# Paired order of the output tiles, and all operand and weight sums on VectorE, in a two-layer decoder trunk

## The chip, the cores and the metric

The kernel runs on one core of a Trainium2 chip. The time is the device time of one execution in microseconds (us). A core has five engines that run their own instructions in order and meet through semaphores: TensorE (PE in the rows, PEld its weight loads), VectorE (DVE), ScalarE (ACT), GpSimd (POOL) and SyncE (SP), which here issues the loads.

## The reference

The reference is a trunk of two pre-norm residual blocks on 512 tokens of width 1024. The first block's mixer is HGRN2 beside retention, the second's is native sparse attention; each mixer ends in an output projection, and each block ends in a SwiGLU layer of hidden width 2816. Cut to what matters here:

```python
for layer in range(2):
    x = x + mixer(rmsnorm(x, g_mix)) @ w_out
    y = rmsnorm(x, g_ffn)
    x = x + (silu(y @ w_gate) * (y @ w_up)) @ w_down
return rmsnorm(x, g_final)
```

Everything is float32.

## The kernel before

All activations lie transposed: the residual stream is eight tiles `h[m]`, each of 128 channels by 512 tokens. To keep float32 accuracy, every operand of a matmul is cut into a high part, cast by ScalarE to the fast fp32r format, and a low part, the rest, which VectorE subtracts; `mm3` then issues three matmuls (high by high, high by low, low by high). Weights are cut in `split` (wh at L77, wl at L78), everything else in `cut` (high at L213, low at L214). Raw weights come by DMA into a ring of three buffers, `raw`; a load is issued only when the tile three loads back has been read by all its readers.

`ffn` does the output projection of the mixer and the SwiGLU layer. First it makes the eight output tiles in the order m = 0 to 7. Each has its own PSUM tile `ps_o`, which TensorE fills by 24 matmuls; VectorE adds it to `h[m]` (L286); `token_side` then makes the operands from the scaled tile, and `square` adds its squares to `acc` for the norm.

The gate and up products follow a scheme of Strassen and Winograd over a 2x2 split of weights and tokens, with seven products for eight. The operands on the token side are b1 and b2 (b3), which are cuts of halves of the scaled tile, and four sums: t1 is the high half of the tokens less the low half, made from tiles 0 to 3 alone, and t3, t2, t4 combine tile m (4 to 7) with tile m − 4. On the weight side, `weight_side` makes four sums s1 to s4 (L259, L260, L262, L264) of the four 128x512 blocks a11, a12, a21, a22 of a hidden tile. There are 22 hidden tiles j per layer, made in groups of 2, 4, 4, 4, 4, 4, and each has its seven products, five reads of these from PSUM (L331, L336, L338, L340 on VectorE and copies on ScalarE), a scaling by the norm (L341 and L342 on GpSimd), the silu (L343), the product with up (L344) and its cut (L347, L348). Between the tiles of one group stand the down projections of the group before, whose results VectorE adds to `h` (L313).

In which order each engine runs its instructions is decided when the program is built: a scheduler simulates the engines and takes the instructions as they become ready. So a change of the engine of one instruction shifts its neighbours too.

GpSimd makes t1 of tiles 0 to 3, the three sums of tile 4, the adds to `acc` for tiles 1 to 4, and all weight sums; VectorE does the rest.

Of the kernel before, what the change touches and what calls it, by code (L numbers as in the profile page):

```python
# [13 lines left out]
ALU = mybir.AluOpType  # L14
# [5 lines left out]
TH = T // 2  # L20
D = 1024
KD = D // P
# [8 lines left out]
NHEAD = 16  # L31
START = "x0 f0 x1 x2 x3 f1 x4 q0 x5 x6 q1 x7"
WARM = 10
BANK_OUT = (0, 3)
OWN_DOWN = (0, 3, 6)
AHEAD = 4
# [15 lines left out]
class Core:  # L52
# [105 lines left out]
    def run(self):  # L158
        tc, nc, io = self.tc, self.nc, self.io
        with tc.tile_pool(name="sp", bufs=1) as sp, tc.tile_pool(name="wp", bufs=1) as wp, \  # L160
# [25 lines left out]
            ps = self.bank(0, "ps_w")  # L186
            for _ in range(WARM):
                nc.tensor.matmul(ps[:, :P], self.ones, self.ones, start=True, stop=True)
# [28 lines left out]
    def token_side(self, m, gain, kept, b):  # L217

        nc, fs = self.nc, self.fs
        g = self.par[:, C_GAIN + 8 * gain + m:C_GAIN + 8 * gain + m + 1]  # L220
        x = fs.tile([P, T], F32, tag=("g", "s", "xg")[min(m // 2, 2)], name="xg", bufs=2)
        nc.scalar.activation(x, self.h[m], AF.Identity, scale=g)
        lo, hi = x[:, :TH], x[:, TH:]
        tr = lambda: fs.tile([P, TH], F32, tag="tr", name="tr", bufs=7)
        if m < 4:
            b[1].append(self.cut("b1", lo, TH, 4))
            t1 = tr()
            nc.gpsimd.tensor_tensor(t1, hi, lo, ALU.subtract)
            b[5].append(self.cut("t1", t1, TH, 4))
            kept.append(x)  # L230
            return
        xh, xl = self.cut("b2", x, T, 4)
        b[2].append((xh[:, :TH], xl[:, :TH]))
        b[3].append((xh[:, TH:], xl[:, TH:]))
        y = kept[m - 4]
        t3, t2, t4 = tr(), tr(), tr()
        eng = nc.gpsimd if m == 4 else nc.vector
        eng.tensor_tensor(t3, hi, y[:, TH:], ALU.subtract)
        eng.tensor_tensor(t2, t3, y[:, :TH], ALU.add)
        eng.tensor_tensor(t4, lo, t2, ALU.subtract)  # L240
        b[7].append(self.cut("t3", t3, TH, 4))
        b[6].append(self.cut("t2", t2, TH, 4))
        b[4].append(self.cut("t4", t4, TH, 4))

    def weight_side(self, j, layer):

        nc, fs = self.nc, self.fs
        raw = []
        for i in range(2):
            w = self.wp.tile([P, WN], F32, tag="raw", name="raw", bufs=3)  # L250
            nc.sync.dma_start(w, self.io["gu"][layer, 2 * j + i])
            raw += [w[:, :WS], w[:, WS:]]
        a11, a12, a21, a22 = raw
        sw = lambda: fs.tile([P, WS], F32, tag="sw", name="sw", bufs=4)
        a = {}
        a[1], = self.split(a11, WS, False)
        a[2], = self.split(a12, WS, False)
        s1, s2, s3, s4 = sw(), sw(), sw(), sw()
        nc.gpsimd.tensor_tensor(s1, a21, a22, ALU.add)  # L259
        nc.gpsimd.tensor_tensor(s2, s1, a11, ALU.subtract)  # L260
        a[5] = self.cut("s", s1, WS, 5)
        nc.gpsimd.tensor_tensor(s3, a11, a21, ALU.subtract)  # L262
        a[6] = self.cut("s", s2, WS, 5)
        nc.gpsimd.tensor_tensor(s4, a12, s2, ALU.subtract)  # L264
        a[7] = self.cut("s", s3, WS, 5)
        a[4], = self.split(a22, WS, False)
        a[3] = self.cut("s", s4, WS, 5)
        return a

    def ffn(self, outs, w_out, gain, layer, next_gain):  # L270
        tc, nc, io, sp = self.tc, self.nc, self.io, self.sp
        with tc.tile_pool(name="fs", bufs=1) as fs, tc.tile_pool(name="fps", bufs=6, space=PSUM) as fps:
            self.fs = fs
            acc = sp.tile([P, T], F32, tag="acc", name="acc", bufs=1)
            b = {i: [] for i in range(1, 8)}
            kept = []
            for m in range(KD):
                ps = self.bank(self.turn + 1 + m // 3, "ps_o") if m in BANK_OUT else \
                    fps.tile([P, T], F32, tag="gu", name="ps_o")
                w = self.weight(w_out[m])  # L280
                if m == BANK_OUT[1] and self.last is not None:
                    with tc.issue_after(self.last):
                        self.dense_t(ps, w, outs)
                else:
                    self.dense_t(ps, w, outs)
                nc.vector.tensor_tensor(self.h[m], ps, self.h[m], ALU.add)  # L286
                self.token_side(m, gain, kept, b)
                self.square(m, self.h[m], acc, m < 5)

            def product(i, a, ps=None):  # L290

                new = ps is None
                if new:
                    ps = fps.tile([P, T], F32, tag="gu", name=f"p{i}")[:, :TH]
                ah, al = a[i]
                for k, (bh, bl) in enumerate(b[i]):
                    c = slice(k * P, (k + 1) * P)
                    self.mm3(ps, ah[:, c], al[:, c], bh, bl, new and k == 0, k == 3, not new)
                return ps
# [17 lines left out]
            for size in GROUPS:  # L317
                hid = []
                for j in range(done, done + size):
# [8 lines left out]
                    y = product(5, a)  # L328
# [30 lines left out]
            acc = sp.tile([P, T], F32, tag="acc", name="acc", bufs=1)  # L359
# [801 lines left out]
```

## Time and profile before

| what | value |
|---|---|
| median of 3 runs | 1341.58 us (1338.67 to 1341.74) |
| the profiled execution | 1340.35 us, its span 1338.2 us |
| mean granted TensorE clock | 0.980 |
| TensorE busy | 1276.7 us (95%) |
| VectorE busy | 1016.4 us (76%), 1829 instructions |
| ScalarE busy | 729.4 us (55%) |
| GpSimd busy | 643.9 us (48%), 569 instructions |

The span runs from the first to the last instruction; the profiled execution's own time is 2.15 us longer. Busy shares are means over stages with different limits: the first layer's mixer runs until about 288 us, its SwiGLU until about 660, the second layer's mixer until about 947, and its SwiGLU to the end.

### The profile page before, as it was taken

The numbers are of one execution on the slowest core, as the hardware profiler recorded it, in microseconds if no ns is written. First come the engines' busy times: TensorE is split into PE (matmuls) and PEld (weight loads), VectorE is DVE, ScalarE is ACT, GpSimd is POOL, SyncE is SP. The second block draws the span as 40 slices with busy tenths as digits, with TensorE's granted clock in tenths as the row PEclk, the third lists the DMA queues.
The fourth block names the chain that finished last, engine by engine and source line by source line (L and its number), as shares of the span: only waits on it lengthen the run. The fifth ranks groups of instructions, "written<-read, shape, count | busy, mean of one in ns | idle before, by whom it ended". The sixth has DMA issues, their size and how long they took to land.

```text
span 1338.2 us, 21839 instructions
## 1 busy us (share of the span) xinstructions
PE 1276.7 (95%) x7846; PEld 1119.7 (84%) x7846; DVE 1016.4 (76%) x1829; ACT 729.4 (55%) x1587; POOL 643.9 (48%) x569
## 2 busy tenths in 40 slices
PE   9999999978999999999988999999799999999995
PEld 7888888868899888989876888877698999988883
DVE  7896764799999677775762888986989987766664
ACT  6655454655544444444554788995654444444444
POOL 3432430165666555553025666764665655555501
PEclk9999999999999999999998999999889999999997
DMA  7222211222233223332322211101123322223321
GB/s 254 84 74 69 79 49 63 79 83 79 84 103 110 95 96 99 107 102 89 104 86 94 72 56 48 48 9 63 51 84 124 98 96 95 95 95 96 103 63 63
DMA packets 44125, 115.13 MB, mean 86 GB/s; under 512 B 4913, under 2 KB 10481, under 8 KB 44017
## 3 DMA queue, kind: packets, MB, share of 16 engines
q1 hardware_dynamic: 43872, 113.69, 26.6%
q8 instruction: 62, 1.02, 0.3%
q14 instruction: 47, 0.38, 0.1%
q10 hardware_dynamic: 144, 0.04, 0.0%
HBM read 111.62 MB, written 2.10 MB: 85 GB/s over the span
## 4 chain that ended last, share of the span: by engine, by line
PE 54%; POOL 15%; DVE 15%; ACT 6%; DMA 6%; issue 5%; POOLq 0%; DVEq 0%; SPq 0%; ACTq 0%
DMA raw<-in_gu 5%; PE p L88 4%; PE p L89 4%; PE p L90 4%; PE ps_e L88 3%; PE ps_e L89 3%; PE ps_e L90 3%; DVE wl L78 3%; POOL sw L262 3%; POOL sw L264 3%; PE ps_d L90 3%; PE ps_d L89 3%; PE ps_d L88 3%; POOL sw L259 3%; POOL sw L260 2%
## 5 line engine op out<-in xcount | busy, mean ns | idle before, releaser
L78 DVE TENSOR_TENSOR wl<-raw,wh 128x512 fp32r<-128x512 f32 (+2 forms) x340 | 285.7, 846 | 51.1 <-ACT wh L77 50.4
L77 ACT CAST wh<-raw 128x512 fp32r<-128x512 f32 (+2 forms) x356 | 211.1, 604 | 179.9 <-PE p L89 44.9
L214 DVE TENSOR_TENSOR sl<-sw,sh 128x512 fp32r<-128x512 f32 x176 | 188.7, 1076 | 19.9 <-ACT sh L213 18.7
L259 POOL TENSOR_TENSOR sw<-raw 128x512 f32<-128x512 f32 x44 | 77.4, 1758 | 238.8 <-DMA raw<-in_gu 187.7
L213 ACT CAST sh<-sw 128x512 fp32r<-128x512 f32 x176 | 108.7, 617 | 118.0 <-PE p L89 80.9
L89 PE MATMUL ps_d<-hl,wh 128*128 128x512 f32 x344 | 136.1, 396 | 0.1
L90 PE MATMUL ps_d<-hh,wl 128*128 128x512 f32 x344 | 135.6, 394 | 0.0
L88 PE MATMUL ps_d<-hh,wh 128*128 128x512 f32 x344 | 135.0, 396 | 0.0
L343 ACT ACTIVATE g<-g 128x512 f32<-128x512 f32 x44 | 27.8, 632 | 135.7 <-POOL g L342 135.4
L344 DVE TENSOR_TENSOR g<-s,g 128x512 f32<-128x512 f32 x44 | 31.8, 722 | 72.1 <-ACT g L343 71.0
L927 POOL TENSOR_SCALAR p<-p,sm 128x128 f32<-128x128 f32 (+3 forms) x128 | 68.7, 557 | 32.5 <-DVE sm L924 11.9
L89 PE MATMUL ps_e<-xl,wh 128*128 128x512 f32 x192 | 76.8, 401 | 0.6 <-DVE xl L108 0.6
L88 PE MATMUL ps_e<-xh,wh 128*128 128x512 f32 x192 | 76.9, 404 | 0.2
L90 PEld LDWEIGHTS ps_d<-hh,wl 128*128 128x128 f32 x344 | 64.5, 188 | 14.8
L90 PE MATMUL ps_e<-xh,wl 128*128 128x512 f32 x192 | 76.5, 400 | 0.0
L918 ACT ACTIVATE p<-p,mx 128x256 f32<-128x256 f32 (+3 forms) x128 | 71.7, 565 | 8.8 <-DVE mx L910 8.3
L264 POOL TENSOR_TENSOR sw<-raw,sw 128x512 f32<-128x512 f32 x44 | 73.0, 1660 | 6.4 <-DVE sl L214 6.4
L89 PEld LDWEIGHTS ps_d<-hl,wh 128*128 128x128 f32 x344 | 64.7, 188 | 13.1 <-DVE hl L348 1.0
L88 PEld LDWEIGHTS ps_d<-hh,wh 128*128 128x128 f32 x344 | 64.5, 188 | 13.0
L262 POOL TENSOR_TENSOR sw<-raw 128x512 f32<-128x512 f32 x44 | 75.0, 1706 | 0.0
L342 POOL TENSOR_TENSOR g<-g,rstd 128x512 f32<-128x512 f32 x42 | 59.8, 1423 | 23.1 <-DVE g L338 23.1
L260 POOL TENSOR_TENSOR sw<-sw,raw 128x512 f32<-128x512 f32 x44 | 65.4, 1487 | 8.6 <-issue 4.8
(345 smaller groups left out, 4249.6 us busy)
## 6 DMA issues: line engine op xcount, KB each, us to landing
raw<-in_gu SPq DMA_DIRECT2D x88, 512.0 KB, 3.7
raw<-in_dn SPq DMA_DIRECT2D x80, 256.0 KB, 2.8
raw<-in_ein SPq DMA_DIRECT2D x22, 512.0 KB, 3.7
raw<-in_oin SPq DMA_DIRECT2D x12, 512.0 KB, 3.7
raw<-in_eout SPq DMA_DIRECT2D x8, 512.0 KB, 3.7
bias<-in_bias SPq DMA_DIRECT2D x16, 256.0 KB, 2.6
raw<-in_oout SPq DMA_DIRECT2D x8, 512.0 KB, 3.5
h<-in_x SPq DMA_DIRECT2D x8, 256.0 KB, 5.4
```

The source lines that it names most:

```text
L77: nc.scalar.copy(wh[:, :m], raw[:, o:o + m])
L78: (nc.gpsimd if pool else nc.vector).tensor_tensor(wl[:, :m], raw[:, o:o + m], wh.bitcast(F32)[:, :m], ALU.subtract)
L88: mm(ps, ah, bh, start=start, stop=False, skip_group_check=more)
L89: mm(ps, ah, bl, start=False, stop=False, skip_group_check=more)
L90: return mm(ps, al, bh, start=False, stop=stop, skip_group_check=more)
L213: nc.scalar.copy(hi, src)
L214: nc.vector.tensor_tensor(lo, src, hi.bitcast(F32), ALU.subtract)
L259: nc.gpsimd.tensor_tensor(s1, a21, a22, ALU.add)
L260: nc.gpsimd.tensor_tensor(s2, s1, a11, ALU.subtract)
L262: nc.gpsimd.tensor_tensor(s3, a11, a21, ALU.subtract)
L264: nc.gpsimd.tensor_tensor(s4, a12, s2, ALU.subtract)
L918: nc.scalar.activation(p, p, AF.Exp, bias=h["mx"][:, t, b:b + 1], scale=-1.0, accum_out=h["sm"][:, t, b:b + 1])
```

## The change

The output tiles go in the order 0, 4, 1, 5, 2, 6, 3, 7, so that each tile above 3 follows its partner; which tiles take the two spare PSUM banks, and which one is held behind the mixer's last instruction, goes by the position instead of m. And GpSimd gives 198 instructions to VectorE: per layer, t1 of four tiles, the three sums of tile 4, the adds to `acc` of four tiles, and four weight sums for each of 22 hidden tiles. GpSimd keeps the scaling at L341 and L342. In the changed kernel lines 34 to 236 have a number higher by one.

```diff
--- before.py
+++ after.py
@@ -31,6 +31,7 @@
 NHEAD = 16
 START = "x0 f0 x1 x2 x3 f1 x4 q0 x5 x6 q1 x7"
 WARM = 10
+OUT_ORDER = (0, 4, 1, 5, 2, 6, 3, 7)
 BANK_OUT = (0, 3)
 OWN_DOWN = (0, 3, 6)
 AHEAD = 4
@@ -225,7 +226,7 @@
         if m < 4:
             b[1].append(self.cut("b1", lo, TH, 4))
             t1 = tr()
-            nc.gpsimd.tensor_tensor(t1, hi, lo, ALU.subtract)
+            nc.vector.tensor_tensor(t1, hi, lo, ALU.subtract)
             b[5].append(self.cut("t1", t1, TH, 4))
             kept.append(x)
             return
@@ -234,10 +235,9 @@
         b[3].append((xh[:, TH:], xl[:, TH:]))
         y = kept[m - 4]
         t3, t2, t4 = tr(), tr(), tr()
-        eng = nc.gpsimd if m == 4 else nc.vector
-        eng.tensor_tensor(t3, hi, y[:, TH:], ALU.subtract)
-        eng.tensor_tensor(t2, t3, y[:, :TH], ALU.add)
-        eng.tensor_tensor(t4, lo, t2, ALU.subtract)
+        nc.vector.tensor_tensor(t3, hi, y[:, TH:], ALU.subtract)
+        nc.vector.tensor_tensor(t2, t3, y[:, :TH], ALU.add)
+        nc.vector.tensor_tensor(t4, lo, t2, ALU.subtract)
         b[7].append(self.cut("t3", t3, TH, 4))
         b[6].append(self.cut("t2", t2, TH, 4))
         b[4].append(self.cut("t4", t4, TH, 4))
@@ -256,12 +256,12 @@
         a[1], = self.split(a11, WS, False)
         a[2], = self.split(a12, WS, False)
         s1, s2, s3, s4 = sw(), sw(), sw(), sw()
-        nc.gpsimd.tensor_tensor(s1, a21, a22, ALU.add)
-        nc.gpsimd.tensor_tensor(s2, s1, a11, ALU.subtract)
+        nc.vector.tensor_tensor(s1, a21, a22, ALU.add)
+        nc.vector.tensor_tensor(s2, s1, a11, ALU.subtract)
         a[5] = self.cut("s", s1, WS, 5)
-        nc.gpsimd.tensor_tensor(s3, a11, a21, ALU.subtract)
+        nc.vector.tensor_tensor(s3, a11, a21, ALU.subtract)
         a[6] = self.cut("s", s2, WS, 5)
-        nc.gpsimd.tensor_tensor(s4, a12, s2, ALU.subtract)
+        nc.vector.tensor_tensor(s4, a12, s2, ALU.subtract)
         a[7] = self.cut("s", s3, WS, 5)
         a[4], = self.split(a22, WS, False)
         a[3] = self.cut("s", s4, WS, 5)
@@ -274,18 +274,18 @@
             acc = sp.tile([P, T], F32, tag="acc", name="acc", bufs=1)
             b = {i: [] for i in range(1, 8)}
             kept = []
-            for m in range(KD):
-                ps = self.bank(self.turn + 1 + m // 3, "ps_o") if m in BANK_OUT else \
+            for i, m in enumerate(OUT_ORDER):
+                ps = self.bank(self.turn + 1 + i // 3, "ps_o") if i in BANK_OUT else \
                     fps.tile([P, T], F32, tag="gu", name="ps_o")
                 w = self.weight(w_out[m])
-                if m == BANK_OUT[1] and self.last is not None:
+                if i == BANK_OUT[1] and self.last is not None:
                     with tc.issue_after(self.last):
                         self.dense_t(ps, w, outs)
                 else:
                     self.dense_t(ps, w, outs)
                 nc.vector.tensor_tensor(self.h[m], ps, self.h[m], ALU.add)
                 self.token_side(m, gain, kept, b)
-                self.square(m, self.h[m], acc, m < 5)
+                self.square(m, self.h[m], acc)
 
             def product(i, a, ps=None):
```

VectorE's order at the end of the first layer's output projection, before, from the last residual add on (L286, m = 7, the first row). Here tr are the sums of operands, t2l, t3l, t4l and b2l their low parts (L214), wl and sl those of weights and weight sums.

```order
L286 TENSOR_TENSOR h<-ps_o,h 128x512
L78 TENSOR_TENSOR wl<-raw,wh 128x512
L240 TENSOR_TENSOR tr<-xg,tr 128x256
L214 TENSOR_TENSOR t2l<-tr,t2h 128x256
L78 TENSOR_TENSOR wl<-raw,wh 128x512
L238 TENSOR_TENSOR tr<-xg 128x256
L120 TENSOR_TENSOR acc<-acc,sq 128x512
L214 TENSOR_TENSOR sl<-sw,sh 128x512
L239 TENSOR_TENSOR tr<-tr,xg 128x256
L214 TENSOR_TENSOR b2l<-xg,b2h 128x512
L214 TENSOR_TENSOR t4l<-tr,t4h 128x256
L214 TENSOR_TENSOR t3l<-tr,t3h 128x256
```

The same place in the changed kernel, from the last residual add on (m = 7, the first row).

```order
L286 TENSOR_TENSOR h<-ps_o,h 128x512
L239 TENSOR_TENSOR tr<-tr,xg 128x256
L121 TENSOR_TENSOR acc<-acc,sq 128x512
L215 TENSOR_TENSOR t3l<-tr,t3h 128x256
L79 TENSOR_TENSOR wl<-raw,wh 128x512
L215 TENSOR_TENSOR b1l<-xg,b1h 128x256
L260 TENSOR_TENSOR sw<-sw,raw 128x512
L262 TENSOR_TENSOR sw<-raw 128x512
L215 TENSOR_TENSOR sl<-sw,sh 128x512
L240 TENSOR_TENSOR tr<-xg,tr 128x256
L229 TENSOR_TENSOR tr<-xg 128x256
L238 TENSOR_TENSOR tr<-xg 128x256
```

Two weight sums (L260, L262) and t1's difference (L229) now stand between the operand sums.

VectorE's order in the steady part of the first layer, before: a hidden tile from its first product read (L331) on; wl<-raw behind L348 is that of a down weight.

```order
L331 TENSOR_TENSOR g<-p_5460,u 128x256
L348 TENSOR_TENSOR hl<-g,hh 128x512
L78 TENSOR_TENSOR wl<-raw,wh 128x512
L214 TENSOR_TENSOR sl<-sw,sh 128x512
L313 TENSOR_TENSOR h<-ps_d,h 128x512
L336 TENSOR_TENSOR s<-p_5434,u 128x256
L78 TENSOR_TENSOR wl<-raw,wh 128x512
L313 TENSOR_TENSOR h<-ps_d,h 128x512
L78 TENSOR_TENSOR wl<-raw,wh 128x512 x2
L338 TENSOR_TENSOR g<-p_5434,u 128x256
L340 TENSOR_TENSOR s<-p_5420,rstd 128x256
L214 TENSOR_TENSOR sl<-sw,sh 128x512
```

The same place in the changed kernel, from L348 (hl<-g) on; the second wl<-raw is that of the second down weight.

```order
L348 TENSOR_TENSOR hl<-g,hh 128x512
L313 TENSOR_TENSOR h<-ps_d,h 128x512
L79 TENSOR_TENSOR wl<-raw,wh 128x512
L259 TENSOR_TENSOR sw<-raw 128x512
L260 TENSOR_TENSOR sw<-sw,raw 128x512
L262 TENSOR_TENSOR sw<-raw 128x512
L215 TENSOR_TENSOR sl<-sw,sh 128x512
L336 TENSOR_TENSOR s<-p_5621,u 128x256
L313 TENSOR_TENSOR h<-ps_d,h 128x512
L79 TENSOR_TENSOR wl<-raw,wh 128x512
L264 TENSOR_TENSOR sw<-raw,sw 128x512
L79 TENSOR_TENSOR wl<-raw,wh 128x512
```

The sums L259, L260, L262 and L264 now stand between the cuts of the down weights and the reads of the products; L259 reads the raw tile whose load is issued after a down weight's wl.

## Rows read from the trace of the kernel before

**Rows 1.** Windows of two stages: length, busy us by engine, clock, DMA.
```profile
200.00:330.00 130.00, 118.92 (x668) 102.37 (x667) 101.76 (x160) 76.09 (x179) 47.43 (x33) 0.97 0.22 70
330.00:660.00 330.00, 324.76 (x2165) 294.85 (x2164) 254.24 (x362) 153.08 (x293) 164.83 (x116) 1.00 0.32 102
```

**Rows 2.** Waits of TensorE between 200 and 330 us.
```profile
PE p L89 <- DVE b2l L214: 4.3, 1, 4.3
PE p L88 <- ACT b2h L213: 2.9, 1, 2.9
```

**Rows 3.** Timeline of TensorE, first SwiGLU: start, duration, instruction, [idle before].
```profile
288.09 0.28 PE L88 MATMUL p<-b1h,wh 128*128 128x256 f32 x1
...
314.78 0.39 PE L88 MATMUL p<-t4h,wh 128*128 128x256 f32 x1 [2.68 <-ACT u L335]
```

**Rows 4.** Window of 10 us in that start.
```profile
295.00:305.00 10.00, 5.69 (x35) 5.57 (x35) 10.00 (x18) 5.63 (x12) 2.76 (x3) 0.66 0.21 66
```

**Rows 5.** Timeline of TensorE, start of the second SwiGLU.
```profile
947.21 0.28 PE L88 MATMUL p<-b1h,wh 128*128 128x256 f32 x1
947.32 0.28 PE L89 MATMUL p<-b1l,wh 128*128 128x256 f32 x1
...
974.09 0.58 PE L88 MATMUL p<-t4h,wh 128*128 128x256 f32 x1 [1.05 <-ACT u L335]
```

**Rows 6.** VectorE in layer 1, first residual add to first product read.
```profile
261.69 0.69 DVE L286 TENSOR_TENSOR h<-ps_o,h 128x512 f32<-128x512 f32 x1 [4.49 <-PE ps_o L90]
...
279.86 1.78 DVE L78 TENSOR_TENSOR wl<-raw,wh 128x512 fp32r<-128x512 f32 x1
...
284.41 0.68 DVE L286 TENSOR_TENSOR h<-ps_o,h 128x512 f32<-128x512 f32 x1
285.01 0.68 DVE L214 TENSOR_TENSOR sl<-sw,sh 128x512 fp32r<-128x512 f32 x1
...
308.15 0.41 DVE L214 TENSOR_TENSOR t4l<-tr,t4h 128x256 fp32r<-128x256 f32 x1
308.49 0.41 DVE L331 TENSOR_TENSOR g<-p,u 128x256 f32<-128x256 f32 x1
```

**Rows 7.** Timeline of GpSimd in layer 1.
```profile
304.88 4.83 POOL L260 TENSOR_TENSOR sw<-sw,raw 128x512 f32<-128x512 f32 x1 [3.49 <-issue]
...
315.60 0.74 POOL L341 TENSOR_TENSOR s<-s,rstd 128x256 f32<-128x256 f32 x1 [1.90 <-DVE s L336]
```

**Rows 8.** Timeline of VectorE in layer 2, the same two ends.
```profile
917.31 0.69 DVE L286 TENSOR_TENSOR h<-ps_o,h 128x512 f32<-128x512 f32 x1 [0.99 <-PE ps_o L90]
...
966.54 0.41 DVE L331 TENSOR_TENSOR g<-p,u 128x256 f32<-128x256 f32 x1
```

**Rows 9.** Timeline of VectorE and GpSimd in the steady part, two hidden tiles.
```profile
467.45 0.42 DVE L331 TENSOR_TENSOR g<-p,u 128x256 f32<-128x256 f32 x1
...
483.58 0.42 DVE L331 TENSOR_TENSOR g<-p,u 128x256 f32<-128x256 f32 x1
...
484.51 0.68 DVE L78 TENSOR_TENSOR wl<-raw,wh 128x512 fp32r<-128x512 f32 x1
...
488.96 1.67 POOL L259 TENSOR_TENSOR sw<-raw 128x512 f32<-128x512 f32 x1 [7.29 <-DMA raw<-in_gu]
...
490.71 1.30 POOL L260 TENSOR_TENSOR sw<-sw,raw 128x512 f32<-128x512 f32 x1
491.32 1.24 DVE L214 TENSOR_TENSOR sl<-sw,sh 128x512 fp32r<-128x512 f32 x1 [0.41 <-ACT sh L213]
...
496.51 1.29 POOL L342 TENSOR_TENSOR g<-g,rstd 128x512 f32<-128x512 f32 x1
...
498.50 0.69 DVE L344 TENSOR_TENSOR g<-s,g 128x512 f32<-128x512 f32 x1 [3.09 <-ACT g L343]
```

**Rows 10.** Timeline of VectorE: the reads of j = 1 and j = 6.
```profile
315.45 0.41 DVE L331 TENSOR_TENSOR g<-p,u 128x256 f32<-128x256 f32 x1
...
384.47 0.41 DVE L331 TENSOR_TENSOR g<-p,u 128x256 f32<-128x256 f32 x1
```

## Prediction

> **What bounds the kernel now.** I read the windows by stage first. Between 330 and 660 us, the steady part of the first layer's SwiGLU, TensorE is busy 324.8 of 330 us at full clock; between 200 and 330, where the mixer ends and the SwiGLU starts, it is busy 118.9 of 130 at clock 0.97 [rows 1]. So a gain can only come from the two starts (one per layer), and a loss from the steady part. The waits of TensorE in that stretch name the last high and low part of the second operand, b2h and b2l: 2.9 and 4.3 us [rows 2]. The timeline shows where this lies. The out-projection ends at 288.09, where the first product starts; the first product on t4 starts at 314.78, after another 2.7 us for a copy [rows 3]. These 26.7 us hold 108 product matmuls (counted in TensorE's order), which in an undisturbed place start 0.11 to 0.12 us apart [rows 5], and the norm's matmul (1 us by my estimate): 13.7 us of work. So 13.0 us are lost: 9.9 in the waits named, most of the rest to the clock, granted at 0.66 in the mean between 295 and 305 [rows 4], behind those waits. Layer 2 looks the same: 947.21 to 974.09 is 26.9 us [rows 5], 13.2 lost.
>
> Why is b2l late? VectorE makes it. Undisturbed, its 128x512 operations start 0.60 us apart (284.41, 285.01) and its 128x256 ones 0.34 (308.15, 308.49) [rows 6]. From the first residual add (261.69) to the first read of a product at L331 (308.49) its order holds 37 and 29 of these: 22.2 + 9.9 = 32.1 us. It took 46.8, with hardly an idle gap: 14.7 us are stretch, as in the wl of 279.86 that took 1.78 us instead of 0.68 [rows 6]. In the steady part one such pair lies open: GpSimd's L260 runs 490.71 to 492.01, VectorE's sl starts at 491.32 and takes 1.24, that is to about 0.55 after GpSimd's end [rows 9]. An operation of VectorE with both inputs in SBUF waits until GpSimd's has ended. The Trainium skill, "SBUF — State Buffer", section "SBUF: two separate sides", says that VectorE and GpSimd share a port pair under an exclusive lock, not a split of bandwidth; the 1.24 us agrees. It also works the other way: GpSimd's L260 at 304.88 took 4.83 us beside a full VectorE [rows 7], and the casts behind it on ScalarE held up the copy for which TensorE waited at 314.78.
>
> **The change part by part.**
>
> *The move to VectorE, at the starts.* In the new order VectorE has 48 and 33 operations from its first residual add to the first L331 (11 and 4 more): 28.8 + 11.2 = 40.0 us. In that stretch GpSimd has nothing left to run, so I cost them without stretch. Layer 1: 261.69 + 40.0 = 301.7 instead of 308.49, 6.8 us earlier. Layer 2: 917.31 + 40.0 = 957.3 instead of 966.54 [rows 8], 9.2 earlier. Bounds: with no stretch and no wait these; with one wait of 0.3 us (a guess) at each of the eight tiles for ScalarE's casts 2.4 later.
>
> *The order 0, 4, 1, 5, ...* By itself it costs and moves no instruction; matmuls of the out-projection are the same 24 per tile, and each of the eight has a PSUM tile of its own, so TensorE ends it at 288.1 as before. It spreads VectorE's work: a pair's t3, t2, t4 need both tiles of a pair, which before came only with tiles 4 to 7, the last four. In the new walk the last residual add (m = 7) comes near 291 and the last b2l near 298.0.
>
> *TensorE at the starts.* I walked its rows against that. Layer 1: 288.1 + 13.7 of work, and waits of 1.7 (b2l), 1.4 (L331 must free a PSUM tile) and 0.8 (copies): t4 starts at 305.7 instead of 314.78, **−9.1**. Layer 2: 947.2 + 13.7 + 2.4 of waits = 963.3 instead of 974.09, **−10.8**. The floor is no wait at all, 301.8 and 960.9: −13 each. The ceiling is a VectorE that brings b2l only at 305 and 963 as before: 0.
>
> *The clock and the ramp.* Shorter pauses remain, and the pauses of before were followed by a granted 0.66 [rows 4]. I give back 1 us per layer (0 to 3). The lead has then to survive the hidden tiles j = 1 to 6, where VectorE makes the weight splits of the next tiles: before, its L331 of j = 1 and j = 6 lie at 315.45 and 384.47 [rows 10], 69.0 us, in which it was full. The new order holds 73 and 26 operations there, 52.6 us; with 1.8 us of waits for a load and 1.55 us per tile of what GpSimd still does, 62.2. From 310.6 (L331 of j = 1 in my walk) this gives 372.8, 11.7 before 384.47, so TensorE sets the pace there and keeps its lead.
>
> *The steady part.* TensorE needs 16.13 us per hidden tile (467.45 to 483.58) [rows 9]. VectorE's new order has 17 and 4 operations per tile on average, 10.2 + 1.35 = 11.55 us; before, 13 and 4, 9.15. New waits come on top. The first sum s1 (L259) waits for its raw tile. The load for it is issued when wl of the first down weight, three loads back in the same ring of buffers, has been read: in the trace that wl ends at 485.19, and GpSimd's L259 starts at 488.96, released by this DMA [rows 9], 3.77 us later. Before, GpSimd waited (7.29 us there) and nobody minded; now VectorE waits with everything behind it: L260, L262, the next sl, the read at L336, and TensorE for the PSUM tile that L336 frees. In the new order 1.2, 1.8, 0 or 1.8 us of other operations lie between the two, so 3.77 − 1.2 = 2.57 on average. Second, L338 on VectorE, L342 on GpSimd (1.29), L343 on ScalarE and L344 on VectorE are a chain; L344 waited 3.09 [rows 9]. Now two sl lie between, themselves held by L342's lock: about 1.3 of stretch and wait. Third, L341 (0.74 alone [rows 7]) costs 0.3, since an add from PSUM mostly covers it. Sum: 11.55 + 2.57 + 1.3 + 0.3 = 15.7, under 16.13. The sums are for the tile after next, so what counts is the throughput. Cost 0 by this sum; as it is 97% full, I give back **2** over the whole (0 to 4).
>
> *Removed from GpSimd:* 176 weight sums of 1.30 us and more [rows 9] and 22 smaller ones, which nothing on TensorE's path waited for in the steady part; no gain there. *SP's queue:* loads into raw buffers that waited for GpSimd's reads of the sums now wait for VectorE's; at the starts these reads come earlier, in the steady part they were never last. No term.
>
> Sum: −9.1 − 10.8 + 2 (clock, two layers) + 2 = −15.9 against the profiled execution's 1340.35 us (span 1338.2): 1324.4. The median shown, 1341.58, is 1.2 above that execution, so I forecast **1325.7**, say 1326.
>
> **The rivals.**
>
> *The lead is eaten, no change.* If in the ramp each of the five tiles pays the load wait in full (2.57 and 1.55 each, 20.6) VectorE needs 52.6 + 20.6 = 73.2 and L331 of j = 6 falls at 383.8, 0.7 before the old place; TensorE, which follows it there, keeps 0.7 of its 9. Twice that: about 1340. For it: VectorE is busy 10.00 of 10 us between 295 and 305 [rows 4], and had no room in the ramp either. Against it: the ramp's loads are issued well ahead in the new order, with buffers freed by earlier sums.
>
> *VectorE becomes the bound, slower.* If s1 waits the full 3.77 each time and L341 and L342 hold VectorE for their whole 0.74 + 1.29, a tile takes 11.55 + 3.77 + 2.03 = 17.35, 1.22 over TensorE's 16.13. About 15 steady tiles per layer: +36.6. Against the gain of 20: 1340.35 + 16.7 + 1.2 = 1358; if a lead of 10 us per layer is used up first, 1338. I take the middle, 1348. It decides where waits and lock together exceed 4.58 per tile (I have 4.17), and costs more than the starts gain above about 5.2. For it: VectorE is only 0.4 us per tile from the point. Against it: TensorE idles hardly at all in the steady part, and the lock's largest users leave GpSimd. The Trainium skill, "Perfetto Trace Analysis", section "Optimizing Scalar/DVE Operations", names the opposite move: with VectorE saturated some of its work may go to ScalarE or GpSimd, with the reservation that the shared port can undo it. By the first half of that rule this change would go this rival's way; by the reservation, which the 14.7 us of stretch bear out, mine.
>
> **How the numbers follow.** My forecast has 0.62, with its own range 1317 to 1334: the floor of both starts (−13 each, no give-back) is 1316, the give-backs at their upper ends and 2.4 us per start give about 1333. The eaten lead has 0.22, the slower rival 0.16. The range should take in the eaten lead and half of the slower one: 1315 to 1348. A measurement here tells 0.3%, 4 us, from no change. Faster by more: 0.62 and a quarter of the eaten lead, 0.67. Within: the rest of it, 0.17. Slower: 0.16.
>
> **What would show it.** Right: TensorE's waits for b2h and b2l go from 7 us to under 2 in layer 1, t4 starts near 306 and 963, and the granted clock between 295 and 305 is above 0.9; VectorE's sl and wl at the starts take 0.68 again; a wait of VectorE's L259 for the load appears, some 2 to 3 us per tile, and L344's falls under 1.5; L331 stays 16.1 apart. Wrong: L331 more than 16.3 apart, or TensorE waiting for sl or for L336 in the steady part (slower rival); L331 of j = 6 near 384 (eaten lead); b2l near 305 as before (no gain at all).

## The result, and the profile after

The changed kernel takes 1310.94 us (median of 4 runs, 1309.04 to 1312.03) against 1341.66: 0.9773 of the time before, with an interval of 0.9753 to 0.9793. That is 30.7 us, about twice the forecast 15.6, and below its range. The profiled execution has a span of 1308.9 us against 1338.2.

The page's first part, and the windows that answer to [rows 1]:

```profile
PE 1270.2 (97%) x7846; PEld 1120.7 (86%) x7846; DVE 1028.2 (79%) x2027; ACT 731.7 (56%) x1587; POOL 332.0 (25%) x371
```

```profile
200.00:330.00 130.00, 125.37 (x711) 107.71 (x710) 100.73 (x195) 78.90 (x187) 7.66 (x6) 0.99 0.24 79
330.00:660.00 330.00, 329.22 (x2176) 300.51 (x2175) 266.18 (x436) 156.65 (x296) 49.31 (x43) 1.00 0.32 100
```

TensorE's idle time in 130 us around the first start fell from 11.1 to 4.6 us. It also fell from 5.2 to 0.8 us in the steady part, where the prediction saw nothing to gain. VectorE took 198 instructions more and is busy only 12 us longer, because its others are stretched less: the low parts of weights (wl) take 0.72 us in the mean instead of 0.85, those of weight sums (sl) 0.85 instead of 1.08.

The start of the first SwiGLU: VectorE's timeline (the ends of [rows 6] and [rows 8]), TensorE's timeline (those of [rows 3] and [rows 5]), its waits between 288 and 318 ([rows 2]), and the window of [rows 4].

```profile
261.01 0.69 DVE L286 TENSOR_TENSOR h<-ps_o,h 128x512 f32<-128x512 f32 x1 [4.49 <-PE ps_o L91]
...
300.97 0.41 DVE L331 TENSOR_TENSOR g<-p,u 128x256 f32<-128x256 f32 x1
...
906.01 0.69 DVE L286 TENSOR_TENSOR h<-ps_o,h 128x512 f32<-128x512 f32 x1 [0.99 <-PE ps_o L91]
...
946.99 0.41 DVE L331 TENSOR_TENSOR g<-p,u 128x256 f32<-128x256 f32 x1
```

```profile
287.42 0.28 PE L89 MATMUL p<-b1h,wh 128*128 128x256 f32 x1
...
308.03 0.39 PE L89 MATMUL p<-t4h,wh 128*128 128x256 f32 x1 [0.86 <-ACT u L335]
...
935.92 0.28 PE L89 MATMUL p<-b1h,wh 128*128 128x256 f32 x1
...
956.41 0.58 PE L89 MATMUL p<-t4h,wh 128*128 128x256 f32 x1 [0.77 <-ACT u L335]
```

```profile
PE p L90 <- DVE t1l L215: 1.0, 1, 1.0
PE p L89 <- ACT u L335: 0.9, 1, 0.9
PE p L89 <- DVE g L331: 0.8, 1, 0.8
PE p L89 <- ACT u L330: 0.8, 1, 0.8
PE p L89 <- ACT u L327: 0.6, 1, 0.6
```

```profile
295.00:305.00 10.00, 7.88 (x43) 6.53 (x42) 10.00 (x23) 5.54 (x12) 0.00 (x0) 0.83 0.27 80
```

From its first residual add to L331 VectorE took 39.96 us in layer 1 and 40.98 in layer 2; the prediction counted 40.0. The waits for b2h and b2l are gone, and five short ones stand in their place, 4.1 us together; three of them are for copies on ScalarE (u). TensorE needs 20.6 and 20.5 us from its first product to t4, where it needed 26.7 and 26.9. The clock between 295 and 305 us is granted at 0.83 in the mean, where the prediction had named more than 0.9 as a sign.

The steady part. First, TensorE's timeline: the first product on t3 of j = 9 and of j = 20 in layer 1, before, and then after.

```profile
434.36 0.28 PE L88 MATMUL p<-t3h,sh 128*128 128x256 f32 x1
...
611.82 0.40 PE L88 MATMUL ps_d<-hh,wh 128*128 128x512 f32 x1
612.41 0.38 PE L88 MATMUL p<-t3h,sh 128*128 128x256 f32 x1 [0.19 <-ACT u L330]
612.63 0.28 PE L89 MATMUL p<-t3l,sh 128*128 128x256 f32 x1
```

```profile
425.60 0.28 PE L89 MATMUL p<-t3h,sh 128*128 128x256 f32 x1
...
599.16 0.28 PE L89 MATMUL p<-t3h,sh 128*128 128x256 f32 x1
```

Eleven tiles took 178.05 us and now take 173.56: 16.19 and 15.78 us each. So 16.13 was not what TensorE needs. What it waited for is in the row of 612.41: the copy u at L330, on ScalarE. From start to start this wait costs more than the 0.19 us of idle time: the matmul starts 0.59 us after the one before, where undisturbed ones of ps_d lie 0.23 apart, and the next one 0.22 later instead of 0.12. That is 0.46 us, once per tile. ScalarE's timeline before, beside the GpSimd rows of [rows 9]:

```profile
497.84 0.63 ACT L343 ACTIVATE g<-g 128x512 f32<-128x512 f32 x1 [4.76 <-POOL g L342]
498.37 0.60 ACT L213 CAST sh<-sw 128x512 fp32r<-128x512 f32 x1
498.88 0.36 ACT L330 COPY u<-p 128x256 f32<-128x256 f32 x1
```

And after, ScalarE's and GpSimd's timelines:

```profile
498.62 0.63 ACT L343 ACTIVATE g<-g 128x512 f32<-128x512 f32 x1 [0.80 <-POOL g L342]
499.15 0.61 ACT L214 CAST sh<-sw 128x512 fp32r<-128x512 f32 x1
499.67 0.36 ACT L330 COPY u<-p 128x256 f32<-128x256 f32 x1
```

```profile
497.29 1.29 POOL L342 TENSOR_TENSOR g<-g,rstd 128x512 f32<-128x512 f32 x1 [2.23 <-DVE g L338]
```

Before, the silu L343 stood 4.76 us at the head of ScalarE's queue, waiting for L342, with the copy behind it. L342 came late because it stood on GpSimd behind L260, L262, L341 and L264, and these behind L259, which had waited 7.29 us for its load [rows 9]. Now GpSimd is free when L338 delivers, and L343 waits 0.80 us here. Over the 11 tiles it waited 4.8 us in the mean before and waits 2.0 now.

The very end. The second half's last residual add (L383) and TensorE's last matmul of the norm, before, and then after:

```profile
1325.35 0.41 DVE L383 TENSOR_TENSOR h<-ps_f,h 128x256 f32<-128x256 f32 x1
...
1326.26 0.76 PE L389 MATMUL pn<-sq,ones 128*128 128x256 f32 x2 [2.94 <-ACT sq L385]
```

```profile
1296.00 0.42 DVE L383 TENSOR_TENSOR h<-ps_f,h 128x256 f32<-128x256 f32 x1 [0.51 <-PE ps_f L91]
1296.23 1.18 PE L389 MATMUL pn<-sq,ones 128*128 128x256 f32 x3
```

Before, that add stood behind the first half's five scaled outputs on VectorE (L399, L397); after, the scheduler put it ahead of them. The diff doesn't touch these lines. From the last matmul of the tiles that are not split in halves, the end takes 17.7 us instead of 21.2.

### The profile page after: what moved, and what is told of

Read it like the earlier page. It is cut to its first block, busy times and chain, and to the rows that moved or that the text cites. A ratio compares the mean times of both kernels' runs of the same rounds, so it can differ in the third digit from the quotient of the medians.

```text
span 1308.9 us, 21707 instructions
## 1 busy us (share of the span) xinstructions
PE 1270.2 (97%) x7846; PEld 1120.7 (86%) x7846; DVE 1028.2 (79%) x2027; ACT 731.7 (56%) x1587; POOL 332.0 (25%) x371
## 3 DMA queue, kind: packets, MB, share of 16 engines
q1 hardware_dynamic: 43872, 113.69, 27.2%
## 4 chain that ended last, share of the span: by engine, by line
PE 60%; DVE 8%; issue 2%; DMA 2%; ACT 2%; POOL 1%; DVEq 0%; ACTq 0%; POOLq 0%
PE p L89 9%; PE p L90 9%; PE p L91 9%; PE ps_d L90 5%; PE ps_d L91 5%; PE ps_d L89 5%; DMA raw<-in_gu 2%; PE po L966 2%; PE pt L935 2%; PE ps_o L89 2%; PE ps_o L91 2%; PE ps_o L90 2%; DVE wl L79 1%; PE ps_q L89 1%; PE ps_q L90 1%
## 5 line engine op out<-in xcount | busy, mean ns | idle before, releaser
L79 DVE TENSOR_TENSOR wl<-raw,wh 128x512 fp32r<-128x512 f32 (+2 forms) x340 | 244.0, 723 | 43.2 <-ACT wh L78 42.1
L214 ACT CAST sh<-sw 128x512 fp32r<-128x512 f32 x176 | 107.6, 618 | 144.4 <-PE p L90 126.4
L341 POOL TENSOR_TENSOR s<-s,rstd 128x256 f32<-128x256 f32 x44 | 38.9, 884 | 510.9 <-DVE s L336 451.7
L215 DVE TENSOR_TENSOR sl<-sw,sh 128x512 fp32r<-128x512 f32 x176 | 146.3, 848 | 6.5 <-ACT sh L214 6.2
L342 POOL TENSOR_TENSOR g<-g,rstd 128x512 f32<-128x512 f32 x42 | 70.9, 1689 | 138.2 <-DVE g L338 114.5
L259 DVE TENSOR_TENSOR sw<-raw 128x512 f32<-128x512 f32 x44 | 30.3, 689 | 65.3 <-DMA raw<-in_gu 65.2
L910 DVE CUSTOM_DVE_ANT_0 p<-ps_s,bias 128x256 f32<-128x256 f32 (+3 forms) x128 | 59.0, 481 | 8.1 <-PE pt L935 4.9
L313 DVE TENSOR_TENSOR h<-ps_d,h 128x512 f32<-128x512 f32 x80 | 54.6, 682 | 6.5 <-PE ps_d L91 6.3
L343 ACT ACTIVATE g<-g 128x512 f32<-128x512 f32 x44 | 27.8, 632 | 53.1 <-POOL g L342 52.9
L950 DVE TENSOR_TENSOR pl<-pt,ph 128x512 fp32r<-128x512 f32 (+2 forms) x96 | 51.5, 549 | 5.9 <-ACT ph L942 5.7
```

Source lines behind the costliest of these rows:

```text
L79: (nc.gpsimd if pool else nc.vector).tensor_tensor(wl[:, :m], raw[:, o:o + m], wh.bitcast(F32)[:, :m], ALU.subtract)
L214: nc.scalar.copy(hi, src)
L215: nc.vector.tensor_tensor(lo, src, hi.bitcast(F32), ALU.subtract)
L342: (nc.vector if j == NF - 1 else nc.gpsimd).tensor_tensor(g, g, r, ALU.mult)
L910: nc.vector.tensor_tensor_reduce(p, h["dst"][:, b - br[0]], h["bias"][:, T - n:], -1.0, 3e38, ALU.add, ALU.min, h["mx"][:, t, b:b + 1])
```

## Where the 29.3 us of span come from

TensorE's timelines, cut at the same instructions, give the whole difference. Start: first product to first product on t4. Mixer: layer 1's last matmul on ps_d to layer 2's first product. End: layer 2's last matmul on ps_d to the last instruction of TensorE or VectorE.

| stretch | before | after | difference |
|---|---|---|---|
| up to the first product | 288.09 | 287.42 | -0.7 |
| start, layer 1 | 26.69 | 20.61 | -6.1 |
| rest of layer 1's SwiGLU | 346.41 | 339.34 | -7.1 |
| layer 2's mixer | 286.02 | 288.55 | +2.5 |
| start, layer 2 | 26.88 | 20.49 | -6.4 |
| rest of layer 2's SwiGLU | 339.20 | 331.07 | -8.1 |
| the end | 21.19 | 17.66 | -3.5 |

The mixer's +2.5 is not an effect that the runs pin down: over the kernels below, in which it is the same code, it took 285.9 to 289.4 us in their profiled executions. The differences of the table add up to 29.4 by rounding.

## The experiments

All are timed against the kernel before on the same chip; over these sessions its median was 1339.5 to 1342.6 us, so the ratio given with each kernel tells more than a difference between two medians of the table. The table holds the median, and out of each profiled execution's TensorE timeline the two starts, the 11 hidden tiles from j = 9 to 20 in each layer, and the end, as defined above. The 11 tiles hold 1188 matmuls before; where the scheduler orders them otherwise, the stretch between the two marks holds one or two matmuls of the down projections more or fewer, 0.23 us each: one more in layer 1 of the changed kernel, two fewer where 171.87 stands.

| kernel | median | start 1 | start 2 | j 9-20, layer 1 | layer 2 | end |
|---|---|---|---|---|---|---|
| before | 1341.66 | 26.7 | 26.9 | 178.05 | 177.39 | 21.2 |
| changed | 1310.94 | 20.6 | 20.5 | 173.56 | 172.24 | 17.7 |
| order alone | 1340.76 | 28.1 | 28.1 | 178.11 | 177.59 | 17.7 |
| engines alone | 1324.86 | 23.7 | 23.5 | 174.48 | 172.16 | 20.4 |
| weight sums alone | 1319.21 | 26.2 | 22.0 | 172.86 | 172.11 | 17.0 |
| token side alone | 1338.75 | 28.6 | 25.1 | 178.24 | 177.21 | 17.7 |
| before, L342 on VectorE | 1328.10 | 26.7 | 27.0 | 172.33 | 172.33 | 20.4 |
| before, four raw buffers | 1336.28 | 29.2 | 25.3 | 172.33 | 172.34 | 17.7 |
| before, early end | 1337.28 | 27.0 | 28.4 | 178.39 | 176.84 | 18.5 |
| changed, GpSimd kept busy | 1346.28 | 37.2 | 38.7 | 172.56 | 172.10 | 17.7 |
| changed, L341, L342 on VectorE | 1307.56 | 19.4 | 20.8 | 171.87 | 172.34 | 20.4 |
| changed, s1 on GpSimd | 1313.81 | 19.4 | 18.3 | 172.33 | 172.33 | 21.8 |
| L341, L342 on VectorE, early end | 1305.25 | 19.4 | 21.0 | 171.87 | 172.33 | 17.0 |
| the same, s1 on GpSimd | 1303.48 | 19.4 | 19.4 | 172.34 | 172.10 | 17.7 |

**The change in parts.** The order alone is the changed kernel with GpSimd's work left there:

```diff
-            for m in range(KD):
+            for i, m in enumerate(OUT_ORDER):
...
```

> Order 0, 4, 1, 5, ... alone; GpSimd keeps all of its sums. My theory now: between the two traces each start (first product to first product on t4) gained 6.1 to 6.4 us, the hidden tiles some 7 to 8 us per layer, the end 3.6 us. The hidden tiles' part comes from the engine, so here they stay 16.13 us apart; the end comes from where the scheduler puts one residual add (L383), and in this kernel's order it stands early, as after the change: -3.6. The starts gain half, 3 us each. Sum: -9 to -10, about 1332 us. Rival (the order alone makes the starts): starts -12.5, end -3.6, about 1325 us. Rival (the order does nothing without the engines): 1338 us.

Measured: 0.9985 (0.9972 to 0.9999). The hidden tiles stay as they were and the end is shorter, as expected, but the starts are 1.4 and 1.2 us longer. TensorE's waits between 287 and 318 say why:

```profile
PE p L89 <- ACT b1h L214: 5.8, 1, 5.8
PE p L90 <- DVE b1l L215: 2.4, 1, 2.4
```

The first product needs b1 of tiles 0 to 3. In the old order the last of these is the fourth tile, in the new one the seventh, and ScalarE and VectorE hand its parts over late. So the order alone doesn't gain half of the starts, as I had expected, but costs a little.

The engines alone keep `range(KD)` and have all 198 instructions on VectorE.

> All 198 instructions on VectorE, tiles in the order 0 to 7. My theory: the hidden tiles gain as in the changed kernel, -7 to -8 us per layer (pitch 15.8 instead of 16.13); the end stays as before, since L383 stands late in this kernel's order; the starts gain half, -3 us each. Sum: -21, about 1321 us. Rival (the paired order is what makes the lead): starts 0, about 1327 us. Rival (the order does nothing): starts -12.5, about 1314 us.

Measured: 0.9874 (0.9852 to 0.9896), 17 us. The starts gain 3.0 and 3.4 us, the 11 tiles 3.6 and 5.2, nearly what they gain in the changed kernel, the end 0.8. So the order is worth about 3 us per start with the engines moved, and costs 1.3 without. Its part at the starts is seen on VectorE: from its first residual add to L331 in layer 1 it has 86 operations here and takes 43.0 us, in the changed kernel 81 and 40.0. The two profiled executions differ by 15.4 us, though: 2.7 lie in the end, and 2.8 and 3.4 in the rest of the SwiGLU layers, mostly before j = 9. What makes these last two was not tried.

Of the engines, first the weight sums:

```diff
-        nc.gpsimd.tensor_tensor(s1, a21, a22, ALU.add)
+        nc.vector.tensor_tensor(s1, a21, a22, ALU.add)
```

(and s2, s3, s4 likewise).

> Only the four weight sums s1 to s4 move to VectorE; order 0 to 7, t1, the sums of tile 4 and the adds to acc stay on GpSimd. My theory: hidden tiles -15 us in all, end -3.6 (L383 stands early), starts -3 each since most of GpSimd's lock there is weight sums: about 1317 us, pitch 15.8. Rival (the token-side move carries the starts, and the sums only the steady part): about 1323 us.

Measured: 0.9835 (0.9809 to 0.9860). Steady tiles and end are as expected, the starts are uneven (0.5 and 4.9 us). Then the rest of the move, without the weight sums:

```diff
-            nc.gpsimd.tensor_tensor(t1, hi, lo, ALU.subtract)
+            nc.vector.tensor_tensor(t1, hi, lo, ALU.subtract)
...
-        eng = nc.gpsimd if m == 4 else nc.vector
+        eng = nc.vector
...
-                self.square(m, self.h[m], acc, m < 5)
+                self.square(m, self.h[m], acc)
```

> Only the token side moves to VectorE (t1, the sums of tile 4, the adds to acc); weight sums stay on GpSimd, order 0 to 7. My theory: pitch 16.13 as before, end -3.6 (L383 stands early), starts within 2 us of before: about 1337 us. Rival (the token side carries the starts): starts -6 each, about 1326 us.

Measured: 0.9974 (0.9959 to 0.9989), of which the early end is 3.5 us; the starts changed by +1.9 and -1.8. The weight sums carry the move: 22.7 us alone. All 198 instructions gain less, 17.0; 3.4 us of that difference are the late end.

**Why the hidden tiles took 16.13 us.** Two kernels take the queue on GpSimd apart and leave the weight sums there, lock and all.

```diff
-                    (nc.vector if j == NF - 1 else nc.gpsimd).tensor_tensor(g, g, r, ALU.mult)
+                    nc.vector.tensor_tensor(g, g, r, ALU.mult)
```

> The kernel before, with the scaling at L342 on VectorE instead of GpSimd; all weight sums stay on GpSimd. My theory of the hidden tiles' 16.13 us: on GpSimd L342 stands behind L260, L262, L341 and L264, which stand behind the load that L259 waits for; the silu L343 waits for L342, and ScalarE's copy at L330, for which TensorE waits, stands behind L343. Without L342 in that queue the 11 hidden tiles from j = 9 to 20 take 173 to 175 us instead of 178, in both layers, and the whole is 8 to 10 us faster: about 1332 us (the end is in the late order, so nothing there). Rival (the lock: VectorE is held up by GpSimd's sums, and TensorE with it): 178 as before, about 1341 us, or more, as VectorE has one operation more per tile.

Measured: 0.9881 (0.9851 to 0.9910). The same two products as above, in this kernel:

```profile
433.14 0.28 PE L88 MATMUL p<-t3h,sh 128*128 128x256 f32 x1
...
605.47 0.28 PE L88 MATMUL p<-t3h,sh 128*128 128x256 f32 x1
```

172.33 us, 15.67 per tile, in both layers. From t4 on, the hidden tiles and down projections gain 6.5 and 5.4 us; of the 14 us that the medians differ by, the profiled execution shows 10. The lock cannot explain this: GpSimd's 176 sums are all still there, and VectorE's wl and sl take 0.86 and 0.90 us in the mean over these tiles of layer 1, where they took 0.86 and 0.96 before. Nor can another order on TensorE: its 1188 matmuls of this stretch come in the same order as before.

```diff
-        raw = self.wp.tile([P, WN], F32, tag="raw", name="raw", bufs=3)
+        raw = self.wp.tile([P, WN], F32, tag="raw", name="raw", bufs=4)
...
-        tr = lambda: fs.tile([P, TH], F32, tag="tr", name="tr", bufs=7)
+        tr = lambda: fs.tile([P, TH], F32, tag="tr", name="tr", bufs=6)
```

> The kernel before with four raw buffers instead of three, and six instead of seven buffers for the operand sums so that it fits. GpSimd keeps all its work; the load that L259 waits for starts earlier. My theory (the load delays the sums, they delay L342): j = 9 to 20 takes 173 to 175 us instead of 178 in both layers, the end gains 3.5 (L383 stands early): about 1329 us. Rival (the lock): 178, and 1338 us from the end alone.

Measured: 0.9945 (0.9926 to 0.9965). Again 172.33 and 172.34 from j = 9 to 20: with the load early, the sums are done before L342 is due, and L343 doesn't wait at all. TensorE's order in this stretch is again the old one, and VectorE's wl and sl are stretched at least as much as before (0.89 and 1.09 us). The total gains only 6 us, as the tiles between j = 1 and 9 took 3.3 and 6.3 us longer; whether the sixth operand buffer or the scheduler's other order there does that was not tried.

**What set the starts.** Here GpSimd does work that nobody waits for, and VectorE's order is row by row that of the changed kernel:

```diff
+                dum = fs.tile([P, T], F32, tag="dum", name="dum", bufs=1)
+                for _ in range(3):
+                    nc.gpsimd.tensor_tensor(dum, self.h[m], self.h[m], ALU.add)
```

> The changed kernel, with GpSimd adding each output tile to itself three times, into a tile that nobody reads: 48 operations of 1.3 us, at the two starts, 31 us of GpSimd each. VectorE's order is that of the changed kernel, row by row, and it waits for none of them. My theory (the lock stretches VectorE, and VectorE sets the starts): VectorE's operations there go from 0.68 to 1.2 to 1.8 us, and first product to first product on t4 goes from 20.6 to 26 to 29 us in both layers: about 1325 us. Rival (the starts gained because results of GpSimd no longer come late, the lock being a side effect): 20.6 as now, 1311 us.

Measured: 1.0028 (1.0014 to 1.0042), 0.3% slower than before. The first start takes 37.2 us:

```profile
287.09 0.28 PE L89 MATMUL p<-b1h,wh 128*128 128x256 f32 x1
...
324.33 0.39 PE L89 MATMUL p<-t4h,wh 128*128 128x256 f32 x1 [0.86 <-ACT u L338]
```

VectorE's timeline from the first residual add to the first read of a product in layer 1 (here L334):

```profile
260.69 0.69 DVE L286 TENSOR_TENSOR h<-ps_o,h 128x512 f32<-128x512 f32 x1 [4.49 <-PE ps_o L91]
...
318.52 0.42 DVE L334 TENSOR_TENSOR g<-p,u 128x256 f32<-128x256 f32 x1
```

The same 81 operations take 57.8 us instead of 40.0. One of VectorE's groups between 261 and 302, in the changed kernel and then in this one:

```profile
L79 DVE TENSOR_TENSOR wl<-raw,wh 128x512 fp32r<-128x512 f32 x15 | 10.1, 681 | 0.0
```

```profile
L79 DVE TENSOR_TENSOR wl<-raw,wh 128x512 fp32r<-128x512 f32 x11 | 11.3, 1034 | 0.0
```

The same operation takes 0.68 us beside an idle GpSimd and 1.03 in the mean beside a busy one, without any dependence between the two. The Trainium skill, "SBUF — State Buffer", section "SBUF: two separate sides", says that the two share a port pair under an exclusive lock, and this run agrees with it. The loss, 16.6 and 18.2 us, is more than twice the 5 to 8 us expected. GpSimd's 24 operations took 35.0 us in the first start.

**The end by itself.**

```diff
+                late = nc.vector.tensor_tensor(h[m][:, c], ps, h[m][:, c], ALU.add)
...
+            with self.tc.issue_after(late.ins):
+                for i in (0, 2, 3, 1):
```

(both halves' matmuls and adds are written ahead of both halves' outputs, which are queued behind the last add.)

> The kernel before, with the very end in the changed kernel's order: the last residual add of the second token half (L383) stands ahead of the first half's scaled outputs on VectorE instead of behind them. Nothing else moves. My theory: the end, from the last down projection on, takes 17.7 us instead of 21.2, so -3.5 us, about 1338.3 us. Rival (the end is shorter in the other kernels because of what they do before it): no change, 1341.8 us.

Measured: 0.9972 (0.9960 to 0.9984), a median of 1337.28 against 1341.34. So this order is worth some 4 us by the medians. Nothing else moved: four places in VectorE's order differ, none on TensorE, ScalarE or GpSimd. The end takes 18.5 us in the profiled execution, which was the slowest of the 12: 2.7 less than before, not the 3.5 expected.

**What the changed kernel leaves.**

```diff
-                    nc.gpsimd.tensor_tensor(s[:, TH:], s[:, TH:], r[:, TH:], ALU.mult)
-                    (nc.vector if j == NF - 1 else nc.gpsimd).tensor_tensor(g, g, r, ALU.mult)
+                    nc.vector.tensor_tensor(s[:, TH:], s[:, TH:], r[:, TH:], ALU.mult)
+                    nc.vector.tensor_tensor(g, g, r, ALU.mult)
```

> The changed kernel with L341 and L342 on VectorE too, so that GpSimd does nothing in the SwiGLU but the last scalings. VectorE then has 18 and 5 operations per hidden tile, 12.5 us, but no lock, and the chain from L338 to L344 is 0.7 us shorter. My theory: TensorE is at its own work already (15.8 us per tile against 15.7 for its matmuls), so j = 9 to 20 stays at 172 to 174; the end loses 3 us (L383 stands late): about 1313 us. Rival (VectorE is the bound in the changed kernel, as waits for the load and lock fill it): j = 9 to 20 rises by 0.5 us per tile or more, about 1325 us.

Measured: 0.9735 (0.9710 to 0.9759), 0.4% under the changed kernel's ratio in spite of the late end; the two intervals still touch. With 12.5 us of operations per tile VectorE is not the bound: 171.87 and 172.34. It still waits 17.4 us for the load in the 11 tiles of layer 1, and TensorE doesn't wait there at all.

```diff
-        nc.vector.tensor_tensor(s1, a21, a22, ALU.add)
+        nc.gpsimd.tensor_tensor(s1, a21, a22, ALU.add)
```

> The changed kernel with s1 (L259) alone back on GpSimd, so that GpSimd and not VectorE waits for the raw tile's load. It tests the wait that I priced at 2.57 us per hidden tile. My theory: TensorE is at its own pace there, the wait costs nothing, and s1 on GpSimd costs something only if it holds up L342: j = 9 to 20 within 2 us of 172 to 174; at the starts s1's lock costs 1 to 3 us each, and the end is in the late order, +3: about 1317 us. Rival (the wait is what keeps the changed kernel's tiles at 15.8 instead of 15.67): j = 9 to 20 falls to 172 in both layers.

Measured: 0.9799 (0.9780 to 0.9819). In layer 1, 173.56 becomes 172.33; in layer 2 there was nothing to win. But the run doesn't take VectorE's wait away, as I had meant it to: L260 now waits for GpSimd's s1. VectorE's waits in the 11 tiles of layer 1, in the changed kernel and then in this one:

```profile
DVE sw L259 <- DMA raw<-in_gu: 27.2, 11, 3.7
```

```profile
DVE sw L260 <- POOL sw L259: 15.7, 11, 3.6
```

TensorE's timeline in the changed kernel shows what the 1.2 us are. One matmul of a down projection lies between the marks there and not here (0.23); the rest goes with two waits for L336, the read behind these sums, of which this is the longer:

```profile
526.44 0.38 PE L89 MATMUL p<-b2h,sh 128*128 128x256 f32 x1 [0.27 <-DVE s L336]
```

Both are gone here. That the wait for the load makes L336 late is argued from VectorE's order; in layer 2 of the changed kernel the same wait, 26.6 us over 11 tiles, costs TensorE nothing. My expectation for the starts had the wrong sign: they are 1.2 and 2.2 us shorter. But the end is late and 4.1 us longer than the changed kernel's, and in layer 2 the tiles from j = 1 to 9 took 115.0 us where the changed kernel takes 110.0.

Two kernels combine these findings. The first has L341 and L342 on VectorE and the end in the early order:

> The changed kernel with L341 and L342 on VectorE too (1307.6 us by itself), and the end in the early order. My theory: both gains add, the end being 2.7 to 3.5 us shorter than with the late order: about 1304 us. Rival (the end's time is not in that order): 1307.5 us.

Measured: 0.9738 (0.9718 to 0.9758), 1305.25 us. The end is 3.4 us shorter than in the same kernel with the late end, but the ratio isn't lower than its 0.9735, and the stretch from t4 to j = 1 in layer 2 took 2.2 us longer in this execution. So the whole doesn't show that both gains add. The second has s1 on GpSimd as well:

> The fastest kernel so far (changed kernel, L341 and L342 on VectorE, the end in the early order: 1305.25 us) with s1 (L259) alone on GpSimd, which then does nothing else in the hidden tiles. Theory: the hidden tiles are at TensorE's own pace in both, j = 9 to 20 at 172; at the starts s1 on GpSimd takes three operations off a full VectorE and its wait for the load too, as in the changed kernel with s1 on GpSimd, where first product to t4 took 19.4 and 18.3 us: 1 to 3 us less than 1305. Rival (each s1 on GpSimd costs VectorE more by the lock than it takes off): 1306 to 1310 us.

Measured: 0.9717 (0.9688 to 0.9746), 1303.48 us, the lowest median: 7.5 us under the changed kernel. The intervals don't tell it from the kernel just before.

## Why the prediction was wrong

**The steady part is the step that failed.** "TensorE needs 16.13 us per hidden tile" took a pitch for a need. The need is 15.67, as the kernels with L342 on VectorE, with four raw buffers and with s1 on GpSimd show in both layers, the first two with TensorE's old order; it could have been worked out: 84 matmuls of products 0.12 us apart and 24 of the down projections (two tiles of 12) 0.234 apart make 15.7. The missing 0.46 us per tile was one wait of TensorE, which the trace puts at 0.2 to 0.3 us of idle time and which costs the whole 0.46 from start to start, and behind it a chain over four engines: load, sums on GpSimd, L342, L343, copy. I had its rows before me, the 7.29 and the 3.09 us among them, and wrote that "nothing on TensorE's path waited for" the sums. From j = 1 to the end of the down projections this gave 6.6 and 7.9 us; the sum had given back 2. The kernels with L342 on VectorE and with four raw buffers show that the queue does it, with VectorE's wl as stretched as before.

**The end was missing from the sum.** Moving instructions changed the scheduler's order far behind them, and one residual add changed places: 3.5 us in the trace of the changed kernel; alone, 2.7 us in the trace and 0.9972 of the time. The prediction said of the order only what moves at the starts and in the steady part.

**The starts: right mechanism, too large a size.** VectorE's 40.0 us came to 39.96 and 40.98, and the run with a busy GpSimd shows that the lock stretches it. But TensorE gained 6.1 and 6.4 us, not 9.1 and 10.8. The term that was too small is its waits. The list puts them at 4.1 us of idle time in layer 1 and 4.5 in layer 2; from start to start they cost 5.1 and 5.5, where the walk had 3.9 and 2.4. The copies on ScalarE alone left TensorE idle for 2.3 us in layer 1, where the walk had 0.8. Matmuls that start 0.2 to 0.3 us apart instead of 0.12 add 1.7 and 1.2 us, with the clock granted at 0.92 and 0.93 in the mean of these two stretches; for this the sum had 1 per layer. And the order did not come free: alone, it made the starts 1.4 and 1.2 us longer.

So the starts gained 12.5 us where the sum had 17.9, and everything else gained 16.8 where the sum had given back 2. The two errors have opposite signs and cancel in part; that the total missed by 13.4 us and not by 18.8 is luck.

**The ramp and the rivals.** The lead was not eaten: L331 of j = 6 came at 373.9 us, where the walk had 372.8. And VectorE did not become the bound. Its wait for the load appeared as priced (27.2 and 26.6 us over the 11 tiles, 2.4 to 2.5 each), and with it a tile still fits: it cost TensorE at most 1.0 us over 11 tiles in layer 1 and nothing in layer 2. Two of the signs that I had named failed, the clock above 0.9 and L331 16.1 us apart. The reservation of the Trainium skill, "Perfetto Trace Analysis", section "Optimizing Scalar/DVE Operations", is that work given to GpSimd may not help because of the shared port. The run with a busy GpSimd agrees: its additions cost VectorE 17.9 us in the first start. The run with s1 there shows no such cost.

Open: how much of the starts' gain comes from VectorE's operations being stretched less and how much from GpSimd's results no longer coming late, as in the 2.7 us wait for the copy at 314.78; why layer 2's mixer took 2.5 us longer in this execution; what slows the tiles before j = 9 in the kernel with four raw buffers; and what the order does in the SwiGLU behind the starts.

## What to carry to other kernels

Work out what the bounding engine needs from the pitch of its own instructions before you call a steady period its bound, and measure a wait from start to start; a few tenths of a us of wait per tile are worth a walk along the queues that deliver to it. A short operation on the critical chain shouldn't share an in-order engine with long work that waits for a load. And where a scheduler orders the program, compare the order to its very end.

## What the hardware showed that I had not expected

The lock between VectorE and GpSimd costs more than I had priced it at: 24 additions of 1.3 us on GpSimd, on which nothing depended, put 16.6 and 18.2 us on the two starts. It holds GpSimd up as well. In the kernel before, in layer 2:

```profile
959.25 8.52 POOL L259 TENSOR_TENSOR sw<-raw 128x512 f32<-128x512 f32 x1 [7.57 <-DMA raw<-in_gu]
```

This sum, 1.3 us by itself, ended 0.8 us after VectorE's run of 17 undisturbed operations, one behind the other from 959.31 to 966.95. So here it was GpSimd that waited. And one operation per hidden tile there, s1, did no harm: with it on GpSimd the starts were 1.2 and 2.2 us shorter, in another order of instructions. How much GpSimd may take beside a full VectorE before it costs more than it takes was not measured.
